# A two-layer decoder trunk on one core: the query projection is cut into portions inside the attention's steps, and a step's two maps are combined one iteration later

## The chip, the core and the metric

The kernel runs on one core of a Trainium2 chip. The core has five engines that run side by side and meet only at semaphores: TensorE (PE in the profile, its weight loads PEld) multiplies matrices into PSUM, VectorE (DVE) and ScalarE (ACT) work element by element and can read PSUM, GpSimd (POOL) works on SBUF alone, and SyncE (SP) issues most DMAs. Each engine takes its instructions in the order in which the program lists them. The metric is the device time of one execution in microseconds (us).

## The reference, cut to what matters

The input is 512 tokens of 1024 numbers in float32. Layer 0 is SwiGLU, a gated convolution, SwiGLU. Layer 1 is SwiGLU, attention, SwiGLU. The change lies in the attention, which has 8 heads of two maps each and works in blocks of 128 queries:

```
q = (xn @ w_q)                                    # 8 heads x 2 maps x 64 columns
s = einsum(q_blk, k) * scale - slope * dist       # masked where dist < 0
p = softmax(s)
a = p[:, :, 0] - lam * p[:, :, 1]                 # the two maps of a head, combined
o = einsum(a, v)
o = o * rsqrt(mean(o*o) + eps) * subln_g * (1 - lambda_init)
mix = o @ w_o
```

## The kernel before, in words

All products keep float32 accuracy by splitting each operand into a high and a low part: a product is hi x hi, hi x lo and lo x hi, three matmuls for each 128 of the inner dimension. A projection of one head over all tokens (`proj`, L336 to L350) is therefore 8 x 3 = 24 matmuls, each 256 columns wide for half of the tokens or 512 for all. Weights come in by DMA as `raw` and are split on ScalarE and VectorE into two rings, `wf` (8 half units) and `wt` (3 whole units). A unit is split when an earlier one is closed.

The stage before the attention is the down projection of the third SwiGLU (L411, tile `y`). A token block's sum `y` becomes the next input through a chain: ScalarE's sum of squares and GpSimd's root (L466 to L471), VectorE's `tmp` and `h` (L480, L481), the same root again, VectorE's two products into `xn` (L503, L504), eight TensorE transposes into `xps` (L509), and a split into `x_hi` (ScalarE, L490) and `x_lo` (VectorE, L491). For the last two of the four blocks this chain runs while the attention already projects queries.

Attention (from L800). `by_halves` projects the queries of heads 0 to 4 into the tiles `qps` (`early = 5`): first the left half of the tokens for all five heads, which needs only blocks 0 and 1, then the right half. `q_done` scales and splits a head's result into the tile `q` on ScalarE (L816) and VectorE (L817). Then come 32 steps, a head and a query block each (step = 4 x head + block). In `iteration(n)` the stages of several steps are emitted together: `combined` of step n - 1 (VectorE, L887 to L891), `transposed` of n - 2 (PE L898, ScalarE L900), `values` of n - 3 (PE L907, then the sum of squares L466), `scores` (PE L856), `biased` (VectorE, L868) and `exps` (ScalarE, L878) of step n, and `normed` of n - 4 (VectorE, L918). `L_COMB = 1` is the delay of the first of them. In steps 0 to 11 a portion of the projection of heads 5, 6 and 7 follows each iteration: a quarter of a head, 6 matmuls of 512 columns, into a half of a PSUM tile named `spare` (in the profile `att_ps`). `spare` is later the place where the normed output of a head, `on`, is transposed (`o_transposes`, PE L927, split by L490 and L491 into `x_hi` and `x_lo`); `OT_AT` lists the steps after which that is emitted. The output projection (`wo`, again L411, tile `y`) follows, and the last iterations are emitted between its matmuls through a list of due times (`later`).

A scheduler orders each engine's instructions of this stage by its own estimate of when they can run, so what stands next to what on an engine is seen from the order, not from the code.

Of the kernel before, what the change touches and what calls it, by code (L numbers as in the profile page):

```python
# [9 lines left out]
F32 = mybir.dt.float32  # L10
F32R = mybir.dt.float32r
BF16 = mybir.dt.bfloat16
I32 = mybir.dt.int32
AF = mybir.ActivationFunctionType
# [5 lines left out]
P = 128  # L20
D = 1024
S = 512
NT = S // P
KT = D // P
NF = 2816 // P
NH = 8
HD = 64
# [13 lines left out]
FIRST = slice(0, 256)  # L41
SECOND = slice(256, 512)
ALL = slice(0, 512)
# [71 lines left out]
def trunk(ctx, tc, x, gu, dn, norm_g, cin, ck, cout, kvg, wk, wv, wq, lamp, subg, wo, out):  # L115
    nc = tc.nc
# [6 lines left out]
    work = ctx.enter_context(tc.tile_pool(name="work", bufs=1))  # L123
# [3 lines left out]
    later = Later()  # L127

    def acc_tile(name):
        return psum.tile([P, 2, 512], F32, tag="acc", bufs=3, name=name)  # L130
# [205 lines left out]
    def proj(o, key, u, xk, cols, ks=range(KT), spread=False):  # L336

        w = weights.get(key, u)  # L340
        n = cols.stop - cols.start
        order = [(k, a, b) for k in ks for a, b in ((0, 0), (0, 1), (1, 0))]
        if spread:
            order = [(k, 0, 0) for k in ks] + [(k, 1, 0) for k in ks[:4]] + [(k, 0, 1) for k in ks] + \
                    [(k, 1, 0) for k in ks[4:]]
        for j, (k, a, b) in enumerate(order):
            c = slice(k % 4 * P, (k % 4 + 1) * P)
            nc.tensor.matmul(o[:, cols], w[k // 4][a][:, c], xk(k)[b][:, cols],  # L348
                             start=((k, a, b) == (0, 0, 0)), stop=((k, a) == (KT - 1, 1)))
            if j % 3 == 2:  # L350
                later.tick(3 * 0.21 * n / 512)

    def close(*key):
        weights.done(*key)
# [160 lines left out]
    def by_halves(jobs, n):  # L515

        later.keep(2)
        for j in jobs[:n]:
            j(FIRST)
        later.keep(0)  # L520
        for j in jobs[:n]:
            j(SECOND)
        for j in jobs[n:]:
            j(ALL)

    def xk_of(xT):
        return lambda k: (xT[0][:, k, :], xT[1][:, k, :])
# [272 lines left out]
    def attention(xT, finish):  # L800
        with tc.tile_pool(name="att", bufs=1, reuse_waits="tile") as pool:
            tiles, qs, ks, vs = {}, {}, {}, {}
            early = 5

            def q_tile(hd):
                if hd >= early:
                    return spare
                if hd // 2 not in tiles:
                    tiles[hd // 2] = acc_tile("qps")
                return tiles[hd // 2][:, hd % 2, :]  # L810

            def q_done(hd):
                close("q", hd)
                ps = q_tile(hd)
                q = pool.tile([P, 2, S], F32R, tag="q", bufs=early, name="q")
                nc.scalar.activation(q[:, 0, :], ps, AF.Copy, scale=-HD ** -0.5)  # L816
                nc.vector.scalar_tensor_tensor(q[:, 1, :], ps, -HD ** -0.5, q[:, 0, :].bitcast(F32),  # L817
                                               ALU.mult, ALU.subtract)
                qs[hd] = q

            def q_job(hd):
                def go(cols):
                    proj(q_tile(hd), "q", hd, xk_of(xT), cols)
                    if cols.stop == S:
                        q_done(hd)
                return go

            def load_k(hd):
                kt = pool.tile([P, 2, S], F32R, tag="k", bufs=2, name="k")
                nc.sync.dma_start(kt.bitcast(F32), kscr[hd])  # L830
                bias = pool.tile([P, S], F32, tag="bias", bufs=2, name="bias")
                nc.gpsimd.tensor_scalar(bias, dist, 2.0 ** -(hd + 1), 0.0, ALU.mult, ALU.add)
                ks[hd] = kt, bias

            def load_v(hd):
                vs[hd] = pool.tile([P, NT, P], F32, tag="v", bufs=2, name="v")
                nc.sync.dma_start(vs[hd], vscr[:, :, hd * P:(hd + 1) * P].rearrange("t p e -> p t e"))

            load_k(0)
            by_halves([q_job(hd) for hd in range(early)], early)  # L840

            tp, misc = tp_tile("att_ps"), acc_tile("att_ps2")
            trs, av, spare = (tp[:, 0, :], misc[:, 1, :]), tp[:, 1, :], misc[:, 0, :]
            on, oT = {}, {}
            steps = [(hd, i) for hd in range(NH) for i in range(NT)]
            st = [{} for _ in steps]

# [34 lines left out]
            def combined(n):  # L882

                w = (steps[n][1] + 1) * P
                s, z = st[n]["s"], st[n]["z"]
                r = small.tile([P, 2], F32, tag="r", bufs=8, name="r")
                nc.vector.reciprocal(r, z)  # L887
                gm = small.tile([P, 1], F32, tag="gm", bufs=4, name="gm")
                nc.vector.scalar_tensor_tensor(gm, z[:, 0:1], r[:, 1:2], nlam, ALU.mult, ALU.mult)
                a = pool.tile([P, S], F32, tag="a", bufs=4, name="a")  # L890
                nc.vector.scalar_tensor_tensor(a[:, :w], s[:, 1, :w], gm, s[:, 0, :w], ALU.mult, ALU.add)  # L891
                st[n]["a"], st[n]["r"] = a, r

            def transposed(n):
                w, tr = (steps[n][1] + 1) * P, trs[n % 2]
                for j in range(w // P):
                    c = slice(j * P, (j + 1) * P)
                    nc.tensor.transpose(tr[:, c], st[n]["a"][:, c], ident)  # L898
                at = pool.tile([P, S], F32, tag="at", bufs=3, name="at")
                nc.scalar.activation(at[:, :w], tr[:, :w], AF.Copy)  # L900
                st[n]["at"] = at

            def values(n):
                hd, i = steps[n]
                o = av[:, i * P:(i + 1) * P]
                for j in range(i + 1):
                    nc.tensor.matmul(o, st[n]["at"][:, j * P:(j + 1) * P], vs[hd][:, j, :],  # L907
                                     start=(j == 0), stop=(j == i))
                r0 = st[n]["r"][:, 0:1]
                rr = small.tile([P, 1], F32, tag="rr", bufs=4, name="rr")  # L910
                nc.gpsimd.tensor_tensor(rr, rstd(o, P, scale=r0), r0, ALU.mult)
                st[n]["rs"] = rr

            def normed(n):
                hd, i = steps[n]
                if hd not in on:
                    on[hd] = pool.tile([P, S], F32, tag="on", bufs=3, name="on")
                nc.vector.scalar_tensor_tensor(on[hd][:, i * P:(i + 1) * P], av[:, i * P:(i + 1) * P],  # L918
                                               st[n]["rs"], sg, ALU.mult, ALU.mult)
                st[n].clear()  # L920

            def o_transposes(hd):
                if "t" not in oT:
                    oT["t"] = new_xT()
                hi, lo = oT["t"]
                for i in range(NT):
                    nc.tensor.transpose(spare[:, i * P:(i + 1) * P], on[hd][:, i * P:(i + 1) * P], ident)  # L927
                split(hi[:, hd, :], lo[:, hd, :], spare)

            N = len(steps)  # L930
            L_COMB = 1
            OT_AT = (12, 13, 17, 21, 25, 29)

            def iteration(n):
                ok = lambda d: 0 <= n - d < N
                if ok(L_COMB):
                    combined(n - L_COMB)
                if ok(L_COMB + 1):
                    transposed(n - L_COMB - 1)
                if ok(L_COMB + 2):  # L940
                    values(n - L_COMB - 2)
                if ok(0):
                    scores(n)
                    biased(n)
                    exps(n)
                if ok(L_COMB + 3):
                    normed(n - L_COMB - 3)

            for n in range(N):
                hd, i = steps[n]  # L950
                if i == 0:
                    if hd + 1 < NH:
                        load_k(hd + 1)
                    load_v(hd)
                iteration(n)
                nq = early + hd
                if nq < NH:
                    proj(q_tile(nq), "q", nq, xk_of(xT), ALL, range(2 * i, 2 * i + 2))
                    if i == NT - 1:
                        q_done(nq)  # L960
                if n in OT_AT:
                    o_transposes(OT_AT.index(n))
            for n in range(N, N + L_COMB + 4):
# [30 lines left out]
    with tc.manual_schedule():  # L994
# [13 lines left out]
        for t in (0, 1):  # L1008
            xn = work.tile([P, D], F32, tag="tmp", bufs=2, name="xn")
            nc.vector.scalar_tensor_tensor(xn, h[t], r[t], g0, ALU.mult, ALU.mult)  # L1010
            ps = (acc_tile if t else tp_tile)("xps").rearrange("p a (b c) -> p (a b) c", c=P)
# [5 lines left out]
        hi, lo = holder["xT"]  # L1017
# [80 lines left out]
```

## Time and profile before

| what | us |
|---|---|
| median of 3 runs (range) | 1868.78 (1866.51 to 1868.93) |
| profiled execution | 1869.11 |
| its span, first to last instruction | 1867.2 |
| TensorE busy in the span | 1849.8 (99%) |
| VectorE, ScalarE, GpSimd busy | 1191.2, 828.4, 549.2 |
| mean granted TensorE clock, share of full | 0.997 |

TensorE is the engine to follow: it is busy nearly all the time, and what shortens the run shortens TensorE's row of work or a gap in it. The end of a matmul in the profile is modelled, so a small gap can hide in a busy share; the start of a matmul is what the argument uses. Rows with [0.59 <-DVE q] say that the engine was idle for 0.59 us before the row and that VectorE's instruction on tile q ended that.

### The profile page before, as it was taken

The numbers are of one execution on the slowest core, as the hardware profiler recorded it, in microseconds if no ns is written. First come the engines' busy times: TensorE is split into PE (matmuls) and PEld (weight loads), VectorE is DVE, ScalarE is ACT, GpSimd is POOL, SyncE is SP. The second block draws the span as 40 slices with busy tenths as digits, with TensorE's granted clock in tenths as the row PEclk, the third lists the DMA queues.
The fourth block names the chain that finished last, engine by engine and source line by source line (L and its number), as shares of the span: only waits on it lengthen the run. The fifth ranks groups of instructions, "written<-read, shape, count | busy, mean of one in ns | idle before, by whom it ended". The sixth has DMA issues, their size and how long they took to land.

```text
span 1867.2 us, 29878 instructions
## 1 busy us (share of the span) xinstructions
PE 1849.8 (99%) x12026; PEld 1680.4 (90%) x12026; DVE 1191.2 (64%) x1863; ACT 828.4 (44%) x1568; POOL 549.2 (29%) x538
## 2 busy tenths in 40 slices
PE   9999999999999999999999999999999999999998
PEld 9999988898889999988978999988876799999886
DVE  6788753654467888634664778743667478888533
ACT  4555543432244555433523455533467445554422
POOL 3455500100014555200330455500213233555100
PEclk9999999999999999999999999999999999999999
DMA  5233242133322233421543232333232122323421
GB/s 202 81 114 108 97 158 91 68 119 112 113 84 75 93 112 112 148 103 46 166 157 118 91 99 105 114 139 109 90 124 76 52 80 91 108 97 114 155 71 45
DMA packets 41690, 197.68 MB, mean 106 GB/s; under 512 B 3664, under 2 KB 8016, under 8 KB 27856
## 3 DMA queue, kind: packets, MB, share of 16 engines
q1 hardware_dynamic: 39760, 189.49, 29.3%
q0 software_dynamic: 1792, 6.29, 0.8%
q8 instruction: 94, 1.54, 0.3%
q14 instruction: 44, 0.36, 0.1%
HBM read 187.38 MB, written 8.39 MB: 105 GB/s over the span
## 4 chain that ended last, share of the span: by engine, by line
PE 95%; DVE 1%; ACT 1%; DMA 1%; issue 1%; POOL 0%; SPq 0%; ACTq 0%; DVEq 0%; POOLq 0%
PE y L411 31%; PE b L363 17%; PE c L363 11%; PE a L363 11%; PE gu L348 10%; PE cz L348 5%; PE b L348 2%; PE kps L348 2%; PE qps L348 1%; PE sc L856 1%; PE xps L509 1%; PE att_ps L907 1%; PE att_ps L348 1%; PE att_ps L898 1%; DMA raw<-gu 0%
## 5 line engine op out<-in xcount | busy, mean ns | idle before, releaser
L226 POOL TENSOR_TENSOR wf<-raw,wf 128x512 fp32r<-128x512 f32 x216 | 282.1, 1306 | 400.9 <-ACT wf L225 399.8
L411 PE MATMUL y<-wf,psp 128*128 128x512 f32 x1344 | 310.2, 389 | 0.0
L411 PEld LDWEIGHTS y<-wf,psp 128*128 128x128 f32 x1344 | 251.7, 188 | 51.9
L246 ACT ACTIVATE wf<-sums 128x512 fp32r<-128x512 f32 x288 | 164.7, 596 | 276.8 <-DVE sums L240 149.1
L185 DVE TENSOR_TENSOR wf<-raw,wf 128x512 fp32r<-128x512 f32 x212 | 145.7, 704 | 176.7 <-ACT wf L183 176.4
L469 POOL TENSOR_SCALAR rb<-ss 128x1 f32<-128x1 f32 x84 | 28.7, 342 | 774.8 <-ACT junk L466 767.0
L183 ACT ACTIVATE wf<-raw 128x512 fp32r<-128x512 f32 x212 | 128.9, 625 | 231.6 <-PE y L411 124.3
L363 PE MATMUL b<-wt,wf 128*128 128x256 f32 x1728 | 231.2, 283 | 0.0
L363 PE MATMUL a<-x_hi,wf 128*128 128x256 f32 x1152 | 230.8, 283 | 0.0
L248 DVE TENSOR_TENSOR wf<-sums,wf 128x512 fp32r<-128x512 f32 x288 | 191.5, 686 | 50.3 <-ACT wf L246 49.9
L411 PE MATMUL y<-wt,psp 128*128 128x512 f32 x960 | 222.5, 389 | 0.0
L363 PEld LDWEIGHTS b<-wt,wf 128*128 128x128 f32 x1728 | 217.7, 192 | 0.2
L411 PEld LDWEIGHTS y<-wt,psp 128*128 128x128 f32 x960 | 179.9, 188 | 37.1
L363 PEld LDWEIGHTS a<-x_hi,wf 128*128 128x128 f32 x1152 | 190.0, 192 | 0.2
L363 PE MATMUL a<-x_lo,wf 128*128 128x256 f32 x576 | 163.0, 283 | 0.0
L491 DVE TENSOR_TENSOR psp<-praw,psp 128x512 fp32r<-128x512 f32 (+1 forms) x126 | 70.2, 560 | 123.3 <-ACT psp L490 122.9
L225 ACT ACTIVATE wf<-raw 128x512 fp32r<-128x512 f32 x216 | 134.8, 624 | 18.9 <-PE gu L348 8.8
L491 DVE TENSOR_TENSOR wt<-raw,wt 128x1024 fp32r<-128x1024 f32 x77 | 96.2, 1256 | 65.4 <-ACT wt L490 65.1
L490 ACT ACTIVATE psp<-praw 128x512 fp32r<-128x512 f32 (+1 forms) x126 | 65.4, 523 | 156.4 <-PE y L411 152.2
L645 POOL TENSOR_TENSOR praw<-su 128x512 f32<-128x512 f32 x72 | 122.4, 1700 | 33.3 <-DVE su L643 24.5
L363 PE MATMUL c<-x_hi,wf 128*128 128x256 f32 x576 | 115.6, 283 | 0.0
L363 PE MATMUL b<-x_hi,wf 128*128 128x256 f32 x576 | 115.4, 283 | 0.0
(169 smaller groups left out, 3512.8 us busy)
## 6 DMA issues: line engine op xcount, KB each, us to landing
raw<-gu SPq DMA_DIRECT2D x87, 1024.0 KB, 4.8
raw<-dn SPq DMA_DIRECT2D x44, 1024.0 KB, 4.8
raw<-cin SPq DMA_DIRECT2D x12, 1024.0 KB, 4.8
raw<-cout SPq DMA_DIRECT2D x4, 1024.0 KB, 4.8
raw<-wk SPq DMA_DIRECT2D x4, 1024.0 KB, 4.8
raw<-wv SPq DMA_DIRECT2D x4, 1024.0 KB, 5.8
kscr<-kk POOLq DMA_DIRECT2D x8, 512.0 KB, 5.5
raw<-wq SPq DMA_DIRECT2D x4, 1024.0 KB, 4.7
```

The source lines that it names most:

```text
L183: nc.scalar.activation(hi, raw[:, a * 512:(a + 1) * 512], AF.Copy)
L185: nc.vector.tensor_tensor(lo, raw[:, a * 512:(a + 1) * 512], hi.bitcast(F32), ALU.subtract)
L225: nc.scalar.activation(hi, plain, AF.Copy)
L226: nc.gpsimd.tensor_tensor(lo, plain, hi.bitcast(F32), ALU.subtract)
L246: nc.scalar.activation(hi, src, AF.Copy)
L248: Sum.pending.append((self, lambda: nc.vector.tensor_tensor(lo, src, hi.bitcast(F32), ALU.subtract)))
L348: nc.tensor.matmul(o[:, cols], w[k // 4][a][:, c], xk(k)[b][:, cols], start=((k, a, b) == (0, 0, 0)), stop=((k, a) == (KT - 1, 1)))
L363: nc.tensor.matmul(o, a[:, c], b, start=(first and k == 0 and b is xh and a is hi), stop=(last and k == 3 and a is lo), skip_group_check=True)
L411: nc.tensor.matmul(y[t][:, c, :], a, w[c][b], start=(f == first[t] and a is ph and b == 0), stop=(f == last[t] and a is pl))
L490: nc.scalar.activation(hi, src, AF.Copy)
L491: nc.vector.tensor_tensor(lo, src, hi.bitcast(F32), ALU.subtract)
L645: nc.gpsimd.tensor_tensor(praws[f], su[:, 0, :], su[:, 1, :], ALU.mult)
```

## The change

`early` goes from 5 to 4, and before the steps only the left half (`FIRST`, 256 columns) of heads 0 to 3 is projected. Their right half (`SECOND`) is cut into 8 portions of 12 matmuls of 256 columns, one after each of steps 0 to 7 (two steps a head); heads 4 to 7 follow whole in 16 portions of 6 matmuls of 512 columns, one after each of steps 8 to 23. All portions use `spare`. `q_done` copies the half that is complete. `L_COMB` goes from 1 to 2, so that `combined` and all that follows it are emitted one iteration later. The normed outputs `on` of heads 0 to 3 are kept in the two tiles of the norm weights (`gpre`, `gpost`) until they are transposed, since `spare` is free only after step 23: `OT_AT` goes from steps 12, 13, 17, 21, 25, 29 to 24, 25, 26, 27, 28, 30.

```diff
-            early = 5
+            early = 4
...
-            by_halves([q_job(hd) for hd in range(early)], early)
+            later.keep(2)
+            for hd in range(early):
+                proj(q_tile(hd), "q", hd, xk_of(xT), FIRST)
+                q_done(hd, q_tile(hd), FIRST)
+            later.keep(0)
...
+            rest = [[(hd, SECOND, k), (hd, SECOND, k + 2)] for hd in range(early) for k in (0, 4)]
+            rest += [[(hd, ALL, k)] for hd in range(early, NH) for k in range(0, KT, 2)]
...
-                    on[hd] = pool.tile([P, S], F32, tag="on", bufs=3, name="on")
+                    if hd < 4:
+                        if hd % 2 == 0:
+                            rows_of[hd] = work.tile([P, 2, S], F32, tag=("gpre", "gpost")[hd // 2], bufs=1, name="on")
+                        on[hd] = rows_of[hd - hd % 2][:, hd % 2, :]
+                    else:
+                        on[hd] = pool.tile([P, S], F32, tag="on", bufs=3, name="on")
...
-            L_COMB = 1
-            OT_AT = (12, 13, 17, 21, 25, 29)
+            L_COMB = 2
+            OT_AT = (24, 25, 26, 27, 28, 30)
...
-                nq = early + hd
-                if nq < NH:
-                    proj(q_tile(nq), "q", nq, xk_of(xT), ALL, range(2 * i, 2 * i + 2))
-                    if i == NT - 1:
-                        q_done(nq)
+                for nq, cols, k in rest.pop(0) if rest else ():
+                    proj(spare, "q", nq, xk_of(xT), cols, range(k, k + 2))
+                    if k == KT - 2:
+                        q_done(nq, spare, cols)
```

What the order shows. TensorE, start of the attention, before: the end of the left halves of heads 2 and 3 and the transposes of the last token block (`xps`), the second of the two groups of eight that fall into the attention; 93 query matmuls stand ahead of it.

```order
L348 MATMUL qps<-x_hi,wt 128x256 x2
L348 MATMUL qps<-x_lo,wt 128x256
L348 MATMUL qps<-x_hi,wt 128x256
L509 MATMUL xps<-ident,xn 128x128 x8
L348 MATMUL qps<-x_hi,wt 128x256
L348 MATMUL qps<-x_lo,wt 128x256
```

The same group of transposes on TensorE now, with the first two score matmuls of step 0 (`sc`) ahead of it.

```order
L348 MATMUL qps<-x_hi,wt 128x256 x2
L348 MATMUL qps<-x_lo,wt 128x256
L348 MATMUL qps<-x_hi,wt 128x256
L856 MATMUL sc<-k,q 128x256 x2
L509 MATMUL xps<-ident,xn 128x128 x8
L348 MATMUL qps<-x_hi,wt 128x256
```

Only 48 query matmuls (heads 0 and 1, left half) stand ahead of the last group now; the group before it, for the third token block, moved from behind 45 query matmuls to behind 32.

TensorE now, end of the first head's portions: the transpose of step 0's map (L898), then the scores of step 2 (384 columns) and of step 3 (512 columns), which are the first to read the right half of head 0's queries.

```order
L348 MATMUL att_ps_12963<-x_hi,wf 128x256 x2
L348 MATMUL att_ps_12963<-x_lo,wf 128x256
L348 MATMUL att_ps_12963<-x_hi,wf 128x256
L898 MATMUL att_ps<-ident,a 128x128
L856 MATMUL sc<-k,q 128x384 x2
L856 MATMUL sc<-k,q 128x512
L856 MATMUL sc<-k,q 128x384 x4
```

Before, those queries were complete before step 0; now one transpose stands between their last matmul and the scores that read them.

TensorE now, steps 26 to 29: transposes of finished heads into `spare` (L932 now, L927 before) between scores (L856), values (L907) and the maps' transposes (L898).

```order
L932 MATMUL att_ps_12963<-ident,on 128x128 x4
L898 MATMUL att_ps<-ident,a 128x128 x2
L856 MATMUL sc<-k,q 128x512 x2
L907 MATMUL att_ps<-v,at 128x128 x2
L856 MATMUL sc<-k,q 128x512 x2
L932 MATMUL att_ps_12963<-ident,on 128x128 x4
L856 MATMUL sc<-k,q 128x512 x2
L856 MATMUL sc<-k,q 128x256 x2
L907 MATMUL att_ps<-v,at 128x128 x3
L856 MATMUL sc<-k,q 128x256 x4
L898 MATMUL att_ps_12963<-ident,a 128x128 x4
```

Five such transposes of heads stand ahead of the last scores in both orders; before they were spread over the scores of steps 15 to 30, now they lie among those of steps 27 to 31.

## Rows read from the trace of the kernel before

**Rows 1.** Stretches (us): busy us (instructions) of PE, PEld, DVE, ACT, POOL; clock, DMA:

```profile
1338.67:1366.54 27.87, 27.87 (x234) 27.64 (x232) 18.92 (x22) 13.34 (x22) 4.84 (x7) 1.00 0.41 139
1366.54:1409.52 42.98, 41.91 (x238) 30.64 (x237) 30.57 (x103) 28.72 (x88) 10.21 (x30) 1.00 0.34 116
1409.52:1423.06 13.54, 11.97 (x80) 8.11 (x79) 11.45 (x45) 11.71 (x40) 5.05 (x14) 1.00 0.26 83
1423.06:1430.08 7.02, 7.02 (x25) 4.80 (x24) 3.66 (x16) 3.64 (x13) 2.21 (x7) 0.51 0.00 0
1430.08:1456.89 26.81, 24.76 (x161) 17.25 (x160) 23.30 (x96) 22.05 (x80) 10.90 (x29) 1.00 0.23 76
```

**Rows 2.** TensorE by line, 1366.54 to 1409.52 (xcount | busy, mean ns | idle):

```profile
L856 PE MATMUL sc<-k,q 64*128 64x256 f32 (+2 forms) x73 | 12.9, 357 | 0.5 <-DVE m L868 0.5
L907 PE MATMUL att_ps<-v,at 128*128 128x128 f32 x42 | 6.9, 292 | 0.0
L898 PE MATMUL att_ps<-ident,a 128*128 128x128 f32 x26 | 4.8, 278 | 0.0
```

**Rows 3.** TensorE by line, 1409.52 to 1456.89:

```profile
L856 PE MATMUL sc<-k,q 64*128 64x256 f32 (+2 forms) x120 | 21.9, 375 | 1.1 <-DVE gm L889 0.4 <-DVE m L868 0.4
L907 PE MATMUL att_ps<-v,at 128*128 128x128 f32 x80 | 14.1, 312 | 0.7 <-DVE on L918 0.4
L898 PE MATMUL att_ps<-ident,a 128*128 128x128 f32 x42 | 9.1, 305 | 1.8 <-DVE on L918 1.0 <-DVE x_lo L491 0.6
L927 PE MATMUL att_ps<-ident,on 128*128 128x128 f32 x20 | 3.8, 311 | 0.0
```

**Rows 4.** Timeline of TensorE, start of the attention (start us, us, what):

```profile
1338.67 0.28 PE L348 MATMUL qps<-x_hi,wf 128*128 128x256 f32 x1
...
1344.06 1.04 PE L509 MATMUL xps<-ident,xn 128*128 128x128 f32 x8
...
1350.68 1.03 PE L509 MATMUL xps<-ident,xn 128*128 128x128 f32 x8
...
1366.33 0.28 PE L348 MATMUL qps<-x_hi,wf 128*128 128x256 f32 x1
1366.54 0.63 PE L856 MATMUL sc<-k,q 64*128 64x256 f32 x6
1367.75 0.39 PE L348 MATMUL qps<-x_hi,wt 128*128 128x256 f32 x1 [0.59 <-DVE q L817]
...
1370.71 0.40 PE L348 MATMUL att_ps<-x_hi,wf 128*128 128x512 f32 x1
...
1374.23 1.15 PE L856 MATMUL sc<-k,q 64*128 64x256 f32 x12
```

**Rows 5.** Timeline of VectorE, chains of the third and last token block:

```profile
1342.37 0.74 DVE L504 TENSOR_SCALAR xn<-xn,rs 128x1024 f32<-128x1024 f32 x1
...
1344.77 1.27 DVE L481 SCALAR_TENSOR_TENSOR h<-tmp,rs,h 128x1024 f32<-128x1024 f32 x1
...
1346.56 1.21 DVE L503 TENSOR_TENSOR xn<-h,gpre 128x1024 f32<-128x1024 f32 x1
...
1348.83 0.74 DVE L504 TENSOR_SCALAR xn<-xn,rs 128x1024 f32<-128x1024 f32 x1
```

**Rows 6.** Timeline of TensorE, the same transposes in an earlier stage:

```profile
942.67 1.09 PE L509 MATMUL xps<-ident,xn 128*128 128x128 f32 x8 [1.62 <-DVE xn L504]
```

**Rows 7.** The stretch around that row, columns as in Rows 1:

```profile
931.00:945.00 14.00, 12.38 (x71) 10.25 (x70) 9.64 (x14) 4.53 (x7) 2.13 (x4) 1.00 0.87 321
```

**Rows 8.** Timeline of TensorE, steps 12 to 15:

```profile
1409.52 0.98 PE L856 MATMUL sc<-k,q 64*128 64x256 f32 x12
1410.91 0.76 PE L856 MATMUL sc<-k,q 64*128 64x384 f32 x5 [0.41 <-DVE gm L889]
...
1414.67 0.66 PE L898 MATMUL att_ps<-ident,a 128*128 128x128 f32 x4 [0.34 <-DVE x_lo L491]
```

**Rows 9.** Timeline of ScalarE, a copy of 256 columns:

```profile
1327.59 0.40 ACT L490 ACTIVATE psp<-praw 128x256 fp32r<-128x256 f32 x1
```

More of the change, by code (lines that the diff above doesn't have):

```diff
@@ L802, in attention @@
             tiles, qs, ks, vs = {}, {}, {}, {}
-            early = 5
+            early = 4
             def q_tile(hd):
-                if hd >= early:
-                    return spare
                 if hd // 2 not in tiles:
@@ L810, in q_tile, with q_done @@
                 return tiles[hd // 2][:, hd % 2, :]
[L812 to L817, printed above, removed]
-                                               ALU.mult, ALU.subtract)
[L819 to L826, printed above, removed]
+            def q_done(hd, ps, cols):
+                if hd not in qs:
+                    qs[hd] = pool.tile([P, 2, S], F32R, tag="q", bufs=early, name="q")
+                hi, lo = qs[hd][:, 0, cols], qs[hd][:, 1, cols]
+                nc.scalar.activation(hi, ps[:, cols], AF.Copy, scale=-HD ** -0.5)
+                nc.vector.scalar_tensor_tensor(lo, ps[:, cols], -HD ** -0.5, hi.bitcast(F32),
+                                               ALU.mult, ALU.subtract)
+                if cols.stop == S:
+                    close("q", hd)
             def load_k(hd):
@@ L839, in attention @@
             load_k(0)
-            by_halves([q_job(hd) for hd in range(early)], early)
+            later.keep(2)
[3 more added lines that the diff above has]
+            later.keep(0)
             tp, misc = tp_tile("att_ps"), acc_tile("att_ps2")
             trs, av, spare = (tp[:, 0, :], misc[:, 1, :]), tp[:, 1, :], misc[:, 0, :]
-            on, oT = {}, {}
+            on, oT, rows_of = {}, {}, {}
+            rest = [[(hd, SECOND, k), (hd, SECOND, k + 2)] for hd in range(early) for k in (0, 4)]
+            rest += [[(hd, ALL, k)] for hd in range(early, NH) for k in range(0, KT, 2)]
             steps = [(hd, i) for hd in range(NH) for i in range(NT)]
```

## The prediction

> **What bounds the kernel now.** I read the page first: TensorE is busy for 99% of the span, so only what shortens its row of work or closes a gap in it can count. Then the busy time by stretch, cut at the attention's borders [rows 1]. The reader is to see three things in the attention from 1366.54 to 1456.89 us. TensorE is idle for 1.07 us while the portions run (42.98 less 41.91), and for 1.57 and 2.05 us after them: 4.69 us in all, which is 0.25% of the run. VectorE and ScalarE are near full in the last two thirds (11.45 and 11.71 us of 13.54), so there the three engines take turns. And in one stretch, 1423.06 to 1430.08, the granted clock is 0.51, the lower level of 1.2 GHz, where all other stretches have 1.00; TensorE got 25 instructions done in 7.02 us. Third, the lines of TensorE in both parts [rows 2, 3], to price a step with portions and one without. Last, the timelines of the start [rows 4, 5].
>
> What a step costs. The 12 steps with portions took 42.98 us. Out of it go the last 24 matmuls of head 4 (1367.75 to 1370.71: 2.96), the wait of 0.59 ahead of them, and 72 portion matmuls of 512 columns at 0.235 us (15 of them from 1370.71 to 1374.23) [rows 4], 16.9 us. That leaves 22.5. The pipeline was filling: 42 value matmuls for 73 score matmuls, against 80 for 120 later [rows 2, 3]; some 6 more at 0.16 us (6.9 / 42) make 23.5, or 1.96 us a step. The 20 steps without portions took 13.54 + 7.02 + 26.81 = 47.37 us. The slow clock cost 2.8 of that: at full clock 241 instructions took 40.35 us, so 25 take 4.2 and not 7.02 [rows 1]. The 20 transposes of finished heads took 3.8 [rows 3]. That leaves 40.8, or 2.04 us a step. So a step without a portion is hardly dearer than one with it, and the portions were hiding little.
>
> **The change part by part.** The sum is made against the profiled execution, 1869.11 us, 0.33 above the median of 1868.78.
>
> Work. The same products remain, but head 4 is now done in 24 matmuls of 512 columns (5.64 us at 0.235) and not in 48 of 256 (5.75 at 0.12): -0.1. A change between scores, which use 64 rows, and anything else costs 0.09 us (0.21 from 1366.33 to 1366.54 against 0.12 between projections [rows 4]). Counted in the order, there are 92 such changes and not 86: +0.5.
>
> The early transposes, which I hold to be the largest new cost. TensorE runs its list in order. Before, 45 query matmuls stood ahead of the third block's transposes (1338.67 to 1344.06) and 93 ahead of the last block's (1350.68). VectorE finished the rows for them at 1343.11 (1342.37 + 0.74) and 1349.57 (1348.83 + 0.74) [rows 5], so neither waited. Now 32 and 48 stand ahead. TensorE reaches the first group at 1338.67 + 32 x 0.12 = 1342.5 and waits 0.6. The group itself takes 0.87 (6.62 us between the two groups less 48 x 0.12), then 16 matmuls 1.9 and two scores with their two changes 0.4: it reaches the last group at 1346.3. VectorE's chain there is a row of its own instructions (h, xn, x_lo, xn times the root), started by the last y, which ends where it ended; the order on VectorE only swaps a weight split with x_lo, and both still lie ahead of the last product. So the rows come at 1349.57 again and TensorE stands still for 3.2 us, with half of the projection's left part queued behind. An earlier stage shows the same: eight such transposes waited 1.62 us for the same VectorE line [rows 6]. Sum +3.8; if the chain ran 1 us earlier or later, 2.8 to 4.8.
>
> The start of the steps. The wait of 0.59 before head 4's last matmuls, for VectorE's copy of a head, goes: -0.6. New is one at step 2: its scores read the right half of head 0's queries, whose last matmul stands one transpose ahead of them. A 256 column copy by ScalarE from these projections isn't in the trace; the nearest is 0.40 us [rows 9], and the transpose covers half. I take +0.4, between 0 (other work is pulled in between) and 1.2 (an exp of the row ahead of the copy). For later heads the half is complete two steps or more before it is read, so nothing waits.
>
> The steps. Twelve more steps get a portion: 12 x (1.96 - 2.04) = -1.0. The nearest bounds are 0 (a portion hides nothing) and -4.1 (all idle time of TensorE in the attention but the 0.59 goes). The later combine gives VectorE one more step before it needs the exponentials; but TensorE's waits there are for VectorE's own turn (gm, m, on, x_lo [rows 3]), so I give it nothing of its own. The splits of the output projection's weights move from the projection stage into steps 1 to 23; there TensorE has 1.4 us of portion in every step, and they are hidden under it: VectorE was busy for 30.57 of 42.98 us in the steps with portions [rows 1]. A unit is 1024 columns, as xn's row of 1.21 us [rows 5], and one falls into each two to four steps; without that cover it would cost 0.3 to 0.6 us a step.
>
> `spare` is handed over 8 times and not 3. The next portion must wait for ScalarE's and VectorE's copies, but an iteration of scores, transposes and values (about 2 us) lies between: 0, up to 0.5 each, 2.5 for the five new ones. The loads on SP's queue (keys, values, raw weights) are issued behind releases that come one iteration later; each still has at least four steps, some 10 us, and nothing is charged. The norm weights now wait for heads 2 and 3 to be transposed and are needed only behind the output projection: nothing.
>
> The transposes of finished heads. As many as before (five) stand ahead of the last scores, but among those of steps 27 to 31. They share one place, and each write waits for the copies of the last. The row to price it: after two of them in a row the next TensorE instruction waited 0.34 us for x_lo [rows 8]. Three or four more of that kind: +1.0, between 0 and 3 (VectorE and ScalarE have little room in such steps).
>
> The clock. Before, it fell once, after 13.5 us without portions. Now that kind of stretch is 8 steps long and not 20. I take it that the clock stays up: -2.8; 0 if it falls again.
>
> Sum: -0.1 + 0.5 + 3.8 - 0.6 + 0.4 - 1.0 + 1.0 - 2.8 = +1.2, so 1870.3 for the profiled run and 1870.0 for the median.
>
> **The rivals.** First, the clock falls here too, in the last 8 steps, which have the same light work as before and more transposes in it. The saving of 2.8 is not made: 1872.8. For it: light steps are where it fell. Against: from 1430.08 to 1456.89 the steps were as light, and the clock stayed at 1.00 [rows 1]. A second way to the same end is the new wait of 3.2 us at the start. In the earlier stage a wait of 1.62 us left the clock at 1.00 [rows 6, 7], and the fall at 1423.06 came after 13.54 us in which TensorE was idle for 1.57 us in all [rows 1], so by the rows one wait alone is not likely to do it. The Trainium skill (page "TensorE: Matmul & The Clock Gate", section "Why this matters for your kernels") holds idle gaps between bursts of matmuls to be what lowers the clock. By that rule the 3.2 us would cost up to half of a stretch like that of 7.02 us, 3.5 us on dense work, and the fall at 1423.06 would not be explained; the row disagrees with it there.
>
> Second, the other side: the portions and the later combine free TensorE. The mechanism is run-ahead: with 1.4 us of independent matmuls in 24 steps, VectorE and ScalarE finish before TensorE asks, and the idle time goes whole. Then the steps give -4.1 and not -1.0, and no crowding remains, because the three engines enter the last steps well ahead (-1.0): 1870.0 - 4.1 = 1865.9, and below 1865.0 if the chain of the last block is 1 us shorter as well. It decides from the point where a step with portion costs 1.8 us or less beside its portion. Against it: 12 steps with portions were there, and cost 1.96.
>
> Third, slower: `spare` binds. If ScalarE and VectorE serve each of the eight copies late because exponentials and weight splits stand ahead, TensorE waits with a portion's first matmul, and the crowded transposes wait likewise: 2.5 + 2 more, with the clock down or not: 1874.5. It would decide from 0.5 us per handover on.
>
> **How the numbers follow.** Forecast 0.45, clock falls 0.27, run-ahead 0.20, `spare` 0.08. A measurement tells a difference from none from about 0.2% on, 3.7 us: below 1865.0 is faster, above 1872.5 slower. The forecast's own range is 1867.5 to 1872.5; of its 0.45 I leave 0.03 for faster and 0.05 for slower. Of the clock's 0.27, 0.20 are slower; of the run-ahead's 0.20, 0.16 faster; of the last 0.08, 0.07 slower. That makes 0.19 faster, 0.49 same, 0.32 slower. The range for 8 in 10 takes in the run-ahead with the shorter chain and the third rival: 1864.5 to 1875.5.
>
> **What would show it.** Right: an idle row of about 3 us of TensorE before the second group of xps, ended by VectorE's line L504; a wait of some tenths before step 2's scores; all stretches at clock 1.00; steps of about 2.0 us beside their portion of 1.4. Wrong: no such idle row (then VectorE's chain came sooner, and the run is some 3 us shorter), steps well under 1.9 us, or a stretch at 0.5. The whole is wrong if the time moves by more than 6 us either way, since all waits of the attention together are hardly more.

## The result and the profile after

The changed kernel takes 1877.6 us (median of 4 runs, 1876.20 to 1878.27) against 1868.09 us before (4 runs, 1866.51 to 1868.93). The ratio is 1.0053 with a 95% interval of 1.0041 to 1.0065: slower by some 9.5 us, about half a per cent, and outside the range given. The profiled execution took 1876.2 us, its span 1874.4.

The loss shows at the start of the attention. The stretches of the changed kernel, which answer to [rows 1] (columns as there: busy time of TensorE, its weight loads, VectorE, ScalarE and GpSimd with their instructions, then the granted clock):

```profile
1338.13:1347.66 9.53, 7.42 (x59) 6.88 (x57) 9.53 (x9) 7.03 (x14) 4.67 (x6) 1.00 0.54 180
1347.66:1357.90 10.24, 5.21 (x23) 4.84 (x24) 5.43 (x9) 1.37 (x2) 1.31 (x2) 0.50 0.33 109
1357.90:1363.59 5.69, 5.31 (x43) 4.97 (x43) 1.90 (x9) 2.82 (x7) 0.00 (x0) 1.00 0.00 0
1363.59:1405.00 41.41, 39.83 (x265) 31.05 (x263) 29.64 (x99) 27.40 (x84) 11.75 (x27) 1.00 0.29 102
1405.00:1448.00 43.00, 41.86 (x227) 30.14 (x227) 27.63 (x100) 27.33 (x93) 15.70 (x39) 1.00 0.31 103
1448.00:1464.83 16.83, 16.02 (x102) 11.17 (x101) 15.12 (x58) 13.85 (x49) 5.58 (x15) 1.00 0.21 62
```

In the first three rows, 25.46 us, TensorE is busy for 17.94: it stands still for 7.5 us where before it stood still for none, and in the second row the clock is at 0.50, the lower level of 1.2 GHz, while TensorE is busy for 5.21 us. In all other stretches the clock is 1.00, the last eight steps included. What TensorE waited for from 1336 to 1475 us (in all, times, longest):

```profile
PE xps L509 <- DVE xn L504: 4.4, 2, 3.9
PE qps L348 <- DVE q L816: 2.7, 1, 2.7
PE sc L856 <- DVE m L868: 1.3, 4, 0.3
PE sc L856 <- ACT q L815: 1.2, 2, 0.9
...
PE att_ps L348 <- DVE q L816: 0.4, 1, 0.4
```

The rows of TensorE's timeline that answer to [rows 4]:

```profile
1342.63 1.09 PE L509 MATMUL xps<-ident,xn 128*128 128x128 f32 x8 [0.51 <-DVE xn L504]
...
1345.57 0.50 PE L856 MATMUL sc<-k,q 64*128 64x256 f32 x2
1349.99 1.94 PE L509 MATMUL xps<-ident,xn 128*128 128x128 f32 x8 [3.92 <-DVE xn L504]
1354.63 0.58 PE L348 MATMUL qps<-x_hi,wt 128*128 128x256 f32 x1 [2.70 <-DVE q L816]
...
1367.89 1.31 PE L856 MATMUL sc<-k,q 64*128 64x384 f32 x7 [0.89 <-ACT q L815]
```

and of VectorE's, which answer to [rows 5]:

```profile
1349.09 0.75 DVE L504 TENSOR_SCALAR xn<-xn,rs 128x1024 f32<-128x1024 f32 x1 [0.72 <-POOL rs L471]
1349.76 2.49 DVE L185 TENSOR_TENSOR wf<-raw,wf 128x512 fp32r<-128x512 f32 x4
1353.03 1.22 DVE L491 TENSOR_TENSOR x_lo<-xps,x_hi 128x1024 fp32r<-128x1024 f32 x1 [0.78 <-ACT x_hi L490]
1354.17 0.41 DVE L816 SCALAR_TENSOR_TENSOR q<-qps,q 128x256 fp32r<-128x256 f32 x1
```

The reader is to see a chain of three. The last block's rows are ready at 1349.84 (1349.09 + 0.75), about when they were before (1349.57), but TensorE is at their transposes by 1346.07. Behind them stands head 1's projection. It writes into the PSUM tile that holds head 0's result (into the other half of it), and it waits for head 0's copy, which is VectorE's last row here: behind four weight splits and the x_lo of the very transposes that came late. And 1.6 us into the first wait the clock falls, for 10.24 us.

The part ahead of the prediction calls the 48 matmuls ahead of the last group heads 0 and 1. They are heads 0 and 2: head 1 shares its tile with head 0 and comes behind the transposes.

### The profile page after: what moved, and what is told of

Read it like the earlier page. It is cut to its first block, busy times and chain, and to the rows that moved or that the text cites. A ratio compares the mean times of both kernels' runs of the same rounds, so it can differ in the third digit from the quotient of the medians.

```text
span 1874.4 us, 29839 instructions
## 1 busy us (share of the span) xinstructions
PE 1851.0 (99%) x12002; PEld 1680.6 (90%) x12002; DVE 1192.8 (64%) x1867; ACT 828.8 (44%) x1572; POOL 554.2 (30%) x538
## 4 chain that ended last, share of the span: by engine, by line
PE 95%; DVE 2%; issue 1%; DMA 1%; ACT 1%; POOL 0%; SPq 0%; ACTq 0%; DVEq 0%; POOLq 0%
PE y L411 31%; PE b L363 17%; PE c L363 11%; PE a L363 11%; PE gu L348 10%; PE cz L348 5%; PE b L348 2%; PE kps L348 2%; PE att_ps L348 2%; PE sc L856 1%; PE att_ps L907 1%; PE xps L509 1%; PE att_ps L898 0%; DMA gpre<-norm_g 0%; PE qps L348 0%
```

## The experiments

Two theories stood at the outset. By the first, the time lost lies in these waits and the clock alone. By the second, the steps cost: portions in 24 of them and the combine one iteration later. "Stretch" is the time from the first query matmul to the first matmul of the last feed-forward part (1338.13 to 1518.00 in the changed kernel); all edits lie inside it, and the clock column counts it alone. Before it, kernels that are alike there differed by up to 3.8 us from one execution to the next (the first query matmul started at 1337.73 to 1341.49; the four latest, from 1340.62 on, had the clock at 0.50 for 3.41 us near 944 us, of which more below), so stretches tell more than single times. The ratio is against runs of the kernel before on the same chip.

| kernel | stretch, us | clock at 0.5 for, us | median, us | ratio (95%) |
|---|---|---|---|---|
| before, first profile | 172.11 | 7.02 | 1868.09 | 1 |
| before again | 169.22 | 0 | 1867.31 | 1.0010 (0.9999 to 1.0021) |
| after | 179.87 | 10.24 | 1877.6 | 1.0053 (1.0041 to 1.0065) |
| after again | 179.37 | 6.84 | 1877.91 | 1.0062 (1.0049 to 1.0075) |
| copies last | 169.89 | 0 | 1867.67 | 1.0003 (0.9993 to 1.0013) |
| other tiles | 179.15 | 10.17 | 1875.0 | 1.0042 (1.0027 to 1.0058) |
| before, copies by halves | 176.98 | 10.24 | 1872.33 | 1.0029 (1.0018 to 1.0040) |
| after, wait filled | 176.45 | 0 | 1872.38 | 1.0029 (1.0019 to 1.0039) |
| after, copies early on VectorE | 172.13 | 3.41 | 1868.94 | 1.0009 (1.0000 to 1.0018) |
| pairs, copies early | 169.59 | 0 | 1867.1 | 1.0007 (0.9998 to 1.0016) |
| copies last, combine early | 167.52 | 0 | 1867.51 | 1.0004 (0.9995 to 1.0013) |
| pairs, copies and combine early | 167.37 | 0 | 1866.0 | 0.9995 (0.9986 to 1.0004) |
| before, combine late | 168.47 | 0 | 1865.03 | 0.9994 (0.9985 to 1.0003) |

**The copies of the four heads put last.**

```diff
             for hd in range(early):
                 proj(q_tile(hd), "q", hd, xk_of(xT), FIRST)
-                q_done(hd, q_tile(hd), FIRST)
             later.keep(0)
+            for hd in range(early):
+                q_done(hd, q_tile(hd), FIRST)
```

> The four first halves of the projection stand together again, and the copies of all four behind them; the portions in the steps, the later combine and the finished heads' transposes stay as in the changed kernel. In the program the two groups of early transposes stand again behind 45 and 93 matmuls of the projection, as before the change. Theory 1 (the start): the time lost lies in the first 25 us alone, in the waits of 3.92 us (last group of transposes, for VectorE's rows), 2.70 us (second head, for VectorE's copy of the first) and the stretch of 10.24 us at clock 0.50 behind the first of them. Then all three go, the clock is 1.00 through the attention, and the time is 1865.5 to 1868.5 us. Theory 2 (the steps): portions in 24 steps and the combine one iteration later are what costs, and the start's waits would come back further on; then the time stays at 1874 us or more.

Theory 1 holds. The start is 13.34 us without a gap, the last transposes stand at 1353.51 with no wait, and the ratio is 1.0003. All other parts of the change are in this kernel, so with this interval (0.9993 to 1.0013) they add up to between 1.3 us gained and 2.4 us lost.

```profile
1341.49:1354.83 13.34, 13.34 (x114) 13.20 (x112) 13.34 (x16) 7.53 (x15) 4.85 (x7) 1.00 0.43 135
```

Of the copies one wait is left, 1.43 us ahead of the first portion, since VectorE has them behind weight splits and x_lo:

```profile
1357.24 0.38 PE L348 MATMUL att_ps<-x_hi,wf 128*128 128x256 f32 x1 [1.43 <-DVE q L816]
```

**Neighbouring heads in different PSUM tiles.**

```diff
-                if hd // 2 not in tiles:
-                    tiles[hd // 2] = acc_tile("qps")
-                return tiles[hd // 2][:, hd % 2, :]
+                if hd % 2 not in tiles:
+                    tiles[hd % 2] = acc_tile("qps")
+                return tiles[hd % 2][:, hd // 2, :]
```

> Only the places of the heads are changed: neighbouring heads lie in different PSUM tiles (0 and 2 in one, 1 and 3 in the other), so that head 1 need not wait for VectorE's copy of head 0. In the program 48 matmuls of the projection stand ahead of the last block's transposes, as in the changed kernel. Theory 1: the wait of 2.70 us goes, the wait of about 3.9 us ahead of the last transposes stays. If a single wait of 3.9 us is enough to lower the clock, it falls here too and the time is 1874 to 1876 us; if it took both waits, the clock stays at 1.00 and the time is 1871 to 1873 us. Theory 2 (the steps): no change, 1877 to 1878 us.

A miss as an experiment on the second wait: with four heads in two tiles somebody has to share with head 0. Now it is head 2, and it waits 2.70 us as head 1 did.

```profile
1349.60 1.94 PE L509 MATMUL xps<-ident,xn 128*128 128x128 f32 x8 [4.37 <-DVE xn L504]
1354.24 0.58 PE L348 MATMUL qps<-x_hi,wt 128*128 128x256 f32 x1 [2.70 <-DVE q L816]
```

But it answers the question on the clock, and the time of 1875.0 us lies in the band for a fall by one wait. The stretch at 0.50 begins at 1349.17, inside the first wait and before the second: one wait was enough.

```profile
1349.17:1359.34 10.17, 7.04 (x32) 6.67 (x33) 4.58 (x8) 1.02 (x1) 0.00 (x0) 0.50 0.30 103
```

**The kernel before with the copies by halves alone.**

```diff
...
                     proj(q_tile(hd), "q", hd, xk_of(xT), cols)
-                    if cols.stop == S:
-                        q_done(hd)
+                    q_done(hd, cols)
```

(The cut part lets `q_done` take a half, as in the changed kernel.)

> The kernel before, with one part of the change alone: each half of a head is copied as soon as it is done, for all five heads and still ahead of the steps. The steps stay as before (portions of heads 5 to 7 in steps 0 to 11, combine one iteration later than the scores). In the program the last block's transposes stand behind 68 matmuls of the projection and not behind 93. Theory 1 (the start): TensorE reaches them about 2 us too early (25 matmuls at 0.12 us are 3.0, of which 1.1 us were slack), so a wait of 1.5 to 2.5 us, and with it 1869.5 to 1871 us; if the clock falls in it as well, 1872 to 1874 us. Theory 2 (the steps): no part of the cost lies here, 1867.5 to 1868.7 us.

This one part of the change, without portions and without the later combine, costs 1.0029, at 1872.33 us inside the band given for waits with a fall of the clock. The order of heads changes as in the changed kernel, and the waits are of the same kinds, only smaller; the clock is at 0.50 for 10.24 us from 1353.27 on, over the transposes and the projection that is queued behind:

```profile
1345.63 1.09 PE L509 MATMUL xps<-ident,xn 128*128 128x128 f32 x8 [0.51 <-DVE xn L504]
...
1351.43 0.50 PE L348 MATMUL qps<-x_hi,wf 128*128 128x256 f32 x2 [1.11 <-DVE wf L185]
...
1352.99 1.69 PE L509 MATMUL xps<-ident,xn 128*128 128x128 f32 x8 [0.58 <-DVE xn L504]
...
1357.38 0.58 PE L348 MATMUL qps<-x_hi,wt 128*128 128x256 f32 x1 [1.85 <-DVE q L818]
```

The profile shows the longest of the ten executions, 1876.41 us, so its stretch of 176.98 us is the bad end and not the middle. Three of the ten had a mean clock of 0.999 and took 1869.37 to 1870.91 us, close to what was given for waits without a fall; the four at 0.997 and below took 1873.14 to 1876.41. As far as mean clocks of whole executions tell, the fall behind the waits came in some executions of this kernel and not in others.

**The changed kernel with its wait filled.**

```diff
...
+                for _ in range(fill):
+                    nc.tensor.matmul(ps[:, 0, :], ident, ident, start=True, stop=True)
                 for k in range(KT):
                     nc.tensor.transpose(ps[:, k, :], xn[:, k * P:(k + 1) * P], ident)
...
```

(`fill` is 14 for the last block ahead of the attention and 0 elsewhere.)

> The changed kernel with 14 products of the identity with itself (float32, two passes of 128 columns each, about 0.12 us a pass, 3.4 us in all) ahead of the last block's transposes, in the place that the transposes then overwrite; nothing else moves. TensorE is busy in most of the wait of 3.92 us. If the idle time is what lowers the clock, it stays at 1.00 and the time is lower by half of the 5.21 us that TensorE was busy in the slow stretch, 2.6 us: 1874 to 1876 us, although the kernel does more. If the clock falls for another reason (the kind of work, as 64-row matmuls and transposes), the slow stretch stays and the time is 1877 to 1878.5 us.

More work, less time: 1.0029 against 1.0053 and 1.0062 for the changed kernel, and 1872.38 us is below both bands that I gave. The last transposes start when they did (11.79 us behind the first query matmul, 11.86 in the changed kernel), and from there everything runs at full clock:

```profile
1347.13 3.39 PE L509 MATMUL xps<-ident 128*128 128x128 f32 x28 [0.63 <-DVE x_lo L491]
1350.36 1.07 PE L511 MATMUL xps<-ident,xn 128*128 128x128 f32 x8
1353.08 0.39 PE L348 MATMUL qps<-x_hi,wt 128*128 128x256 f32 x1 [1.65 <-DVE q L819]
```

```profile
1347.13:1357.72 10.59, 8.56 (x68) 7.98 (x69) 7.37 (x14) 3.69 (x7) 2.14 (x2) 1.00 0.41 137
```

The eight transposes take 1.07 us and not 1.94. Head 1 waits 1.65 us and not 2.70, but not by the clock alone: something else did move. On VectorE head 0's copy stands ahead of the last block's x_lo here, and behind it in the changed kernel:

```profile
1352.61 0.42 DVE L819 SCALAR_TENSOR_TENSOR q<-qps,q 128x256 fp32r<-128x256 f32 x1
1352.94 1.21 DVE L491 TENSOR_TENSOR x_lo<-xps,x_hi 128x1024 fp32r<-128x1024 f32 x1
```

The stretch is 3.4 us shorter (179.87 less 176.45). In the changed kernel x_lo held the copy back by 1.14 us (1353.03 to 1354.17); by that estimate some 1.1 us belong to the order and 2.3 to the clock, near the half of 5.21 us that I had expected. That the idle time lowers the clock here does not hang on this: the mean clock was 0.998 or 0.999 in all ten executions, against 0.995 to 0.997 in all eight of the changed kernel.

**Both kernels once more.**

> The kernel before, word for word, profiled once more. In its profile a stretch of 7.02 us from 1423.06 us had the clock at 0.51, which cost 2.8 us, and the run with the copies of the heads put last had no such stretch, yet its time was that of before (ratio 1.0003). Theory 1: the fall belongs to the 20 steps without a portion and comes in every execution; then it is here again, at about 1423 us, and the first query matmul to the first matmul of the last feed-forward part takes 172 us. Theory 2: it comes in some executions only; then this profile has the clock at 1.00 through the steps, that stretch takes 169 to 170 us, and the portions of the changed kernel save next to nothing in the steps.

The same instructions, without the fall. The row of the stretch that was slow in [rows 1], now with 47 instructions where the slow one had 25:

```profile
1423.06:1430.08 7.02, 7.02 (x47) 5.02 (x46) 5.68 (x22) 5.17 (x21) 2.52 (x8) 1.00 0.14 41
```

So the fall at 1423 us belonged to that execution, not to the kernel, and 169.22 us is the stretch to compare with. The price of 2.8 us was right (172.11 less 169.22 is 2.89). Of the 82 executions of the kernel before that were timed beside the experiments, 63 had a mean clock of 0.999, the others 0.996 to 0.998. The ratio of 1.0010 for a kernel against itself also shows that a tenth of a per cent is not told apart here.

> The changed kernel, word for word, profiled and timed once more. If its waits at the start lower the clock each time, the stretch at 0.50 is here again, about 10 us long and right behind the wait of 3.9 us, the stretch from the first query matmul to the last feed-forward part takes 179 to 180.5 us, and the time is 1875.5 to 1878 us. If the fall came by chance, as that of the kernel before did, the clock stays at 1.00 and the stretch takes 176 to 177.5 us.

The same waits (4.4 us in all for the rows, 2.7 for head 0's copy) and the fall are there again, the fall 6.84 us long and not about 10, as I had expected; it begins a little later, behind the long wait and ahead of head 1's.

```profile
1353.32:1360.16 6.84, 4.14 (x21) 3.87 (x19) 2.92 (x5) 1.02 (x1) 0.00 (x0) 0.50 0.43 153
```

The same profile shows the earlier stage of [rows 6] again, and there too the clock falls right behind the wait:

```profile
943.04 1.31 PE L509 MATMUL xps<-ident,xn 128*128 128x128 f32 x8 [2.07 <-DVE xn L504]
943.76:947.17 3.41, 3.41 (x12) 2.73 (x11) 3.26 (x4) 1.02 (x1) 0.53 (x1) 0.50 0.38 154
```

All kernels are alike in that place. In four of the thirteen profiles the wait took 2.05 to 2.66 us, and each had this stretch at 0.50; in the other nine it took 0.81 to 1.62 us, and the clock stayed at 1.00.

**The copies where they were, but early in VectorE's row.**

```diff
-                q_done(hd, q_tile(hd), FIRST)
+                with tc.high_priority():
+                    q_done(hd, q_tile(hd), FIRST)
```

> The changed kernel, each head's first half still copied as soon as it is done and in the same two PSUM tiles, but the copies stand early in VectorE's row: head 0's copy behind the third block's rows and not behind the last block's x_lo. In the program head 1 therefore follows head 0 sooner, and the last block's transposes stand behind 72 matmuls of the projection and not behind 48. Theory (copies between heads that share a tile cost because VectorE serves them late, which in turn puts the transposes early): the waits of 3.92 and 2.70 us shrink to 1.5 us or less together, the clock stays at 1.00, the stretch from the first query matmul to the last feed-forward part takes 170 to 172 us, and the time is 1866.5 to 1869.5 us. Rival (copies between the heads cost by themselves): above 1873 us.

The time is the theory's, 1868.94 us, though the clock still fell, against what I expected, for 3.41 us at the end of a wait of 1.72:

```profile
1351.11 1.75 PE L509 MATMUL xps<-ident,xn 128*128 128x128 f32 x7 [1.72 <-DVE x_lo L491]
```

```profile
1351.08:1354.49 3.41, 3.38 (x16) 3.38 (x17) 2.86 (x9) 0.57 (x3) 0.00 (x0) 0.50 0.28 61
```

In the code the copies stand between the same projections as in the changed kernel. What made them cost 7.7 us more there (179.87 less 172.13) is their place in VectorE's row, with the order on TensorE that follows from it: 72 matmuls ahead of the last group, not 48.

**The combine, early and late, and the two best edits together.** In the run with the copies last:

```diff
-            L_COMB = 2
+            L_COMB = 1
```

and in the kernel before the other way round, 1 to 2.

> The run with the copies of the four heads put last, and the two maps combined one iteration after the scores, as before the change, and not two. The portions in 24 steps stay. If the later combine is worth something beside the portions, TensorE waits more for VectorE's products in the steps: 2 to 4 us slower than with it, 1869 to 1871 us. If, as predicted, it is worth nothing, 1866 to 1868 us.

> The kernel before with the later combine alone; the projection stays where it was. If the later combine is worth something, it is here, where 20 steps run without a portion: the idle time of TensorE in these steps (1.57 and 2.05 us in two stretches) falls, and the time is 1864 to 1866 us. If it is worth nothing, 1866.5 to 1868.5 us. If it costs (four more iterations' rows are open, buffers come free later), above 1869 us.

The times do not tell any of these from the kernel before, so neither expected gain nor expected loss is shown; 1865.03 us lies in the band for a gain, but its interval takes in 1. In the profiles the late combine beside portions makes the stretch 2.4 us longer (169.89 against 167.52), all of it behind the last scores: 55.28 against 52.82 us to the last feed-forward part. From the first scores to the last both take the same (101.28 and 101.37), although with the early combine TensorE waits for VectorE's copies ahead of a portion four times, 3.8 us in all; the first, of 1.4 us, is there with the late combine as well, and the other three, about 0.8 us each, are the third rival's mechanism. In the kernel before, without so many portions, the late combine shortens the stretch by 0.75 us. One profile each; whether 2 us of it are real stays open.

The two pairs of heads, each with its copies behind it and early in VectorE's row:

```diff
-            for hd in range(early):
-                proj(q_tile(hd), "q", hd, xk_of(xT), FIRST)
-                q_done(hd, q_tile(hd), FIRST)
+            for pair in ((0, 1), (2, 3)):
+                for hd in pair:
+                    proj(q_tile(hd), "q", hd, xk_of(xT), FIRST)
+                for hd in pair:
+                    with tc.high_priority():
+                        q_done(hd, q_tile(hd), FIRST)
```

> The changed kernel with the first halves done in pairs: heads 0 and 1, their copies, heads 2 and 3, their copies, the copies ahead of the weight splits in VectorE's row. No head of a pair has to wait for a copy, and the transposes stand behind 45 and 93 matmuls again. With the copies all at the end, the first portion waited 1.43 us and later a transpose 0.60 us, both for VectorE's copies, which stood behind four weight splits. Theory 1 (the order on VectorE makes these waits): both go, the stretch from the first query matmul to the last feed-forward part takes 167.5 to 168.5 us in place of 169.9, and the time is 1863.5 to 1866 us. Rival: the copies push the last rows or the weight splits back, and as much is lost there: 1866 to 1868 us.

The rival holds, at 1867.1 us: the wait of 1.43 us for the copy went, but the first portion now waits for x_lo and x_hi of the last block instead (0.9 and 0.2 us), and a transpose still waits 0.61 us for a copy.

> The two edits that gave the shortest stretches, together: the first halves in pairs with their copies early in VectorE's row, and the two maps combined one iteration after the scores, as before the change. The portions in 24 steps stay. The combine one iteration later made the end longer by 2.4 us in the profile (55.3 against 52.8 us from the last scores on). Expected stretch 167 to 168 us, against 169.2 in the repeated profile of the kernel before: 1864 to 1866.5 us, a ratio of 0.998 to 1.000. If more than 169 us, the waits for `spare` (3.8 us in the run with the copies last and the early combine) are the price of the early combine beside portions.

The stretch is the shortest of all, 167.37 us, and the ratio 0.9995 (0.9986 to 1.0004): as fast as the kernel before, not shown to be faster.

## Why the prediction was wrong

Against the profile of the kernel before without a fall, the changed one loses 10.65 us in the stretch (179.87 less 169.22). The wait of some 3 us ahead of the second group came as forecast, but so did two of the prediction's own signs of being wrong: a stretch at 0.5, and a time that moved by more than 6 us. Three steps failed, the second, third and fourth of this list, and all concern the start or the clock.

- **The early transposes (+3.8)** were sized well as far as they went: 0.51 + 3.92 = 4.4 us. TensorE reached the last group at 1346.07 (forecast 1346.3), and the rows came at 1349.84 (forecast 1349.57).
- **What is queued behind them** was not followed to its end. I wrote that "half of the projection's left part" stands behind, and charged nothing more. Head 1 needs the tile half beside head 0's, and the copies that free it are on VectorE behind the x_lo of the late transposes: 2.70 us more, and 0.38 ahead of the first portion. This is the largest missed term of the sum, and the program's order showed it: heads 0 and 2 before head 1, and a wait for VectorE on head 1's first matmul. I had read the 48 as heads 0 and 1, and then nothing is left behind that shares a tile with head 0.
- **"By the rows one wait alone is not likely to do it"** was wrong. The clock fell in or right behind the wait of 3.92 us. The slow stretch cost half of its 5.21 us of busy time, 2.6, and some 2.3 by the experiment that filled the wait; the rival's "up to" 3.5 held as a bound. I had argued from one row, a wait of 1.62 us without a fall [rows 6, 7], and from a fall without such a wait [rows 1]. The row was the longest of nine without a fall: at 2.05 us and more in the same place the clock fell in all four profiles. The rule of the Trainium skill that I set against it (page "TensorE: Matmul & The Clock Gate", section "Why this matters for your kernels": idle gaps between bursts of matmuls lower the clock) gave the right answer here, and the filled wait agrees with it: the clock stayed at 1.00 there.
- **"The clock stays up: -2.8"** was a gain that the kernel could not make. In the last eight steps the clock did stay at 1.00, but it does in the kernel before as well when that is profiled again. The credit came from one execution, and the median did not hold it: the mean clock was 0.999 in 63 of 82 executions.
- **The scores of step 2 (+0.4)** waited 0.89 us for ScalarE's copy; the old wait of 0.59 went as forecast. "For later heads ... nothing waits" was not quite so: scores waited once more for such a copy, 0.35 us at 1374.82.
- **The steps, the crowding, `spare`, the moved weight splits**, in sum nothing: right in sum, while no run shows each by itself. With the copies put last the stretch is 0.7 us longer than before, and the copies' own waits in it are 1.43 and 0.60.

The sum, mended: +1.2 without the credit of 2.8 is +4.0; then +0.6 for the transposes, +3.1 for head 1 and the first portion, +2.6 for the clock, +0.8 for the scores' waits, together 11.1 against 10.65 in the profiles and 9.5 and 11.6 in the medians. It is a reckoning after the fact, with terms from the profile that it is held against. The run-ahead did not come: TensorE is still idle for 3.5 us in the steps (1.58, 1.14 and 0.81 in the last three stretches). And `spare` did not bind: the 0.38 us are the only wait for a copy ahead of a portion.

## What to carry to other kernels

Two heads that share a PSUM tile are tied to each other's copies, and a copy emitted between them lets a scheduler reorder everything around: look at the place of that copy in the copying engine's row, and put copies behind the last write of the tile or ahead of the long work on that engine. When a new wait of TensorE comes out at more than a microsecond or two (here 1.72 to 4.37 us), add the price of the lower clock for the work behind it as a case of its own. Profile the kernel before twice, and look at the mean clock of its timed executions, before a stretch at a lower clock is counted as something to be saved.

## What the runs showed of the hardware

- All five profiles (of four kernels) with waits of TensorE of 1.1 us and more ahead of the last transposes ran at 0.50 there, for 3.41 to 10.24 us; the kernel whose wait was filled with useless products did not.
- In an earlier stage, the same in all kernels, waits of 2.05 to 2.66 us were followed by 3.41 us at 0.50 in all four profiles that had them, waits of 0.81 to 1.62 us in none of nine. But the length of one wait does not decide alone: the fall at 1423 us had no wait above 0.41 us in the 13.54 us ahead of it.
- 28 passes of the identity, 3.39 us of TensorE, made the changed kernel faster by a quarter to a third of a per cent (1.0029 against 1.0053 and 1.0062); about a third of what the stretch gained is an estimate for the copy that came earlier on VectorE.
- The same kernel showed a stretch of 7.02 us at 0.51 in one profile and none in another, with the same instructions around it, and its mean clock over 82 executions ran from 0.996 to 0.999.
